# Output projection of two attention layers in column groups of 256, 256 and 512 instead of 512 and 512

## The chip, the cores and the metric

The kernel runs on one core of one Trainium2 chip. The metric is the time of one execution on the device, in microseconds (us); the time before is the median of 3 runs, 1074.47 us (1072.22 to 1074.48). The engines of the core are called PE (TensorE, matrix products), DVE (VectorE), ACT (ScalarE), POOL (GpSimd) and SP (SyncE, which issues the loads).

## What is computed

A trunk of four residual layers over 512 tokens of width 1024 in float32: a gated short convolution, a sparse attention, a latent attention and once more the convolution. Each layer is x + Mixer(RMSNorm(x)). What the change touches is the last line of the two attentions, the product of the gated attention output (512 x 1024) with a 1024 x 1024 matrix:

```python
def reference(x, positions, ...):
    for i in range(DEPTH):                       # DEPTH = 4
        kind, j = i % N_MIXERS, i // N_MIXERS    # 0 conv, 1 sparse, 2 latent, 0 conv
        ...
        x = x + y

def dsa_mixer(xn, positions, w_in, q_norm, k_norm, w_out):
    q, k, v, z, qi, ki, wi = jnp.split(xn @ w_in, cuts, axis=-1)
    ...                                          # top-k keys per query, 16 heads of 64
    p = jax.nn.softmax(logits, axis=-1)
    o = jnp.einsum("qhk,qkhd->qhd", p, v_sel)
    ...
    return (o * jax.nn.silu(z)) @ w_out

def mla_mixer(...):
    ...                                          # 16 heads, chunk-causal softmax attention
    return (o * jax.nn.silu(z)) @ w_out
```

## The kernel before

The residual stream lies transposed in SBUF, as eight tiles `X[k]` of 128 features x 512 tokens. A float32 product is made of three matmuls on operands split in two (`hi`, `lo`): `products` (L274 to L276) issues hi x hi, lo x hi and hi x lo. The weights come from HBM as `raw` tiles (three buffers), are split by `convert` (ACT writes `whi`, L153, then POOL writes `wlo`, L155) into four buffers each, and are used once per bank of the group of columns that they belong to.

`features` computes one group of output columns: for each k-tile of 128 input features it issues three matmuls into each of the group's PSUM banks (128 output features x 512 tokens per bank), and when the last k-tile is done, `finish` takes the banks away; for the output projection that is `residual`, which adds a bank to its `X[f]` on DVE. `project_out` goes through the column groups of a projection and asks `banks_of` for four banks per group. There are eight banks: two with the tag `pj` (projections), two with `pt` (turned probabilities), a double one with the tag `s` (scores), and one each with `o` (the mix of probabilities and values) and `tr` (transposes). A weight tile of a group of 512 columns holds one k-tile, one of 256 columns holds two (`Group.per`), so each conversion covers 128 x 512 elements in either case. One projection is 8 k-tiles x 8 blocks x 3 = 192 matmuls named `po`.

The attentions go over eight pairs of heads, and each pair over four blocks of 128 queries, in the steps `scores` (PE into the `s` banks, then DVE masks them and takes the extreme `mn`, L622, ACT takes the exponentials, L625), `normalise` (POOL for one head of the pair, L640, ACT for the other, L642), `turn` (PE transposes into `pt`, L652, ACT or DVE copies back, L657, L655) and `mix` (PE into `o`, L673). A `Filler` lets PE do projections of later pairs between these steps; the last of it are the gate columns 6 and 7, whose products (`pz`) use the `pj` banks. The mix of pairs 0 to 5 is multiplied by its gate on the way out of PSUM; pairs 6 and 7 go to `plain` and are multiplied on POOL when their gates are there (L890, L1066). Then `branch_out` splits the eight gated tiles into `xh` and `xl` (L715, L716) and calls `project_out`. Its eight k-tiles are the eight pairs, so k-tiles 6 and 7 wait for the last two pairs.

The program is written in this order, but a scheduler places the instructions on each engine by its own simulated timeline: a `po` product may stand between steps of the attention if its operands and its bank are free by then. On the chip each engine takes its instructions in the order of this list and waits for semaphores.

Of the kernel before, what the change touches and what calls it, by code (L numbers as in the profile page):

```python
# [69 lines left out]
def encoder(ctx: ExitStack, tc: tile.TileContext, a, out, depth=4):  # L70
# [23 lines left out]
    def bank(name, tag):  # L94
        return ps.tile([P, S], F32, name=name, tag=tag, bufs=BANKS[tag])

    def two_banks(name):

        b = ps.tile([P, 2, S], F32, name=name, tag="s", bufs=1)
        return [b[:, 0], b[:, 1]]  # L100

    def banks_of(name, which):

        if which % 2 == 0:
            return [bank(name, "pj") for _ in range(2)] + two_banks(name)
        return [bank(name, tag) for tag in ("pt", "pt", "o", "tr")]
# [113 lines left out]
    def run(*gens):  # L220
        for g in gens:
            for _ in g:
                pass
# [62 lines left out]
    def features(group, act, finish, banks):  # L286

        for k0, u in units(group):
            for j, w in enumerate(u):
                k = k0 + j  # L290
                x = act(k)
                for i, b in enumerate(banks):
                    c = i * P
                    n = min(P, group.n - c)
                    products(b[:n], [t[:, c:c + n] for t in w], x, k == 0, k == group.nk - 1)
            yield
        for i, b in enumerate(banks):
            finish(i, b)
# [118 lines left out]
    def residual(f, b, last):  # L417
        if last:
            o = wk("out")
            dve.tensor_tensor(o, b, X[f], op=OP.add)  # L420
            nc.sync.dma_start(out[:, f, :], o)
        else:
            dve.tensor_tensor(X[f], b, X[f], op=OP.add)

    def project_out(groups, act, last=False):
        f = 0
        for i, g in enumerate(groups):
            nb = g.n // P
            banks = banks_of("po", i + 1) if nb == 4 else [bank("po", ["pj", "pt"][i % 2])]
            run(features(g, act, lambda j, b, f=f: residual(f + j, b, last), banks))  # L430
            f += nb


    def layer_a(j, last):
# [35 lines left out]
        for f in range(8):  # L470
# [7 lines left out]
            if f == 1 and j == 0 and depth > 1:  # L478
                TAB["sc"] = angles()
        project_out(a[f"a_out{j}"], lambda k: G[k], last)  # L480


# [226 lines left out]
    def branch_out(groups, G, last):  # L709

        act = []
        for x in G:
            hi = tile_of("xh", "xh", dtype=F32R)
            lo = tile_of("xl", "xl", dtype=F32R)
            act_e.activation(hi, x, AF.Copy)  # L715
            dve.tensor_tensor(lo, x, hi.bitcast(F32), op=OP.subtract)  # L716
            act.append((hi, lo))
        project_out(groups, lambda k: act[k], last)
# [381 lines left out]
def _rows(w, cols):  # L1100

    w = w[:, cols]
    return np.ascontiguousarray(w.reshape(w.shape[0] // P, P, w.shape[1]).transpose(1, 0, 2))


def _cols(v):
    return v.reshape(-1, P).T


def pack(inputs):  # L1110
    f = {k: np.asarray(v) for k, v in inputs.items()}
    arr = {}
    arr["x"] = _rows(f["x"][0].T, slice(None))
    arr["pos"] = np.ascontiguousarray(f["positions"][0].reshape(NT, P).T)
    arr["inv"] = np.ascontiguousarray(np.broadcast_to(np.array(INV, np.float32), (P, 32)))
    arr["ident"] = np.eye(P, dtype=np.float32)
    conv = [_cols(np.ascontiguousarray(f["a_conv_w"][j])) for j in range(2)]
    arr["gains"] = np.ascontiguousarray(np.concatenate(
        [_cols(f["a_norm"][0]), _cols(f["b_norm"][0]), _cols(f["c_norm"][0]), _cols(f["a_norm"][1]),
         conv[0], conv[1], _cols(f["a_conv_b"][0]), _cols(f["a_conv_b"][1]),  # L1120
         _cols(f["c_q_lat_norm"][0]), _cols(f["c_kv_lat_norm"][0])], axis=1))
    arr["rows"] = np.concatenate([f["b_q_norm"][0], f["b_k_norm"][0], f["c_q_norm"][0], f["c_k_norm"][0]])[None]
    groups = {}

    def put(name, w, cols):
        arr[name] = _rows(w, cols)
        return name

    def outs(name, w, last=False):
        g = [put(f"{name}_0", w, slice(0, 512))]  # L1130
        if last:
            return g + [put(f"{name}_1{j}", w, slice(512 + P * j, 640 + P * j)) for j in range(4)]
        return g + [put(f"{name}_1", w, slice(512, 1024))]

    for j in range(2):
        w = f["a_w_in"][j]
        groups[f"a_in{j}"] = [
            put(f"a_in{j}_{i}", w, np.concatenate([np.arange(P) + D * b + P * i for b in range(4)]))
            for i in range(8)]
        groups[f"a_out{j}"] = outs(f"a_out{j}", f["a_w_out"][j], last=j == 1)  # L1140
    w = f["b_w_in"][0]
    for n, c in (("q", 0), ("k", 1024), ("v", 2048)):
        groups["b_" + n] = [put(f"b_{n}_{i}", w, slice(c + 256 * i, c + 256 * i + 256)) for i in range(4)]
    groups["b_z"] = [put(f"b_z_{i}", w, slice(3072 + P * i, 3200 + P * i)) for i in range(8)]
    groups["b_idx"] = [put("b_idx_0", w, slice(4096, 4416)), put("b_idx_1", w, slice(4416, 4680))]
    w = f["c_w_in"][0]
    cq = np.arange(384)
    groups["c_lat"] = [put("c_lat_0", w, np.concatenate([np.arange(384, 640), cq[:256]])),
                       put("c_lat_1", w, np.concatenate([cq[256:], np.arange(640, 672)]))]
    groups["c_z"] = [put(f"c_z_{i}", w, slice(672 + P * i, 800 + P * i)) for i in range(8)]  # L1150
    groups["c_uq"] = [put(f"c_uq_{i}", f["c_w_uq"][0], slice(384 * i, 384 * i + 384)) for i in range(4)]
    groups["c_ukv"] = [put(f"c_ukv_{i}", f["c_w_ukv"][0], slice(512 * i, 512 * i + 512)) for i in range(4)]
    groups["c_out"] = outs("c_out", f["c_w_out"][0])
    groups["b_out"] = outs("b_out", f["b_w_out"][0])
    return arr, groups


# [25 lines left out]
```

## Time and profile before

| | us |
|---|---|
| median of 3 runs (lowest to highest) | 1074.47 (1072.22 to 1074.48) |
| the profiled execution, its own time | 1078.64 |
| its span, first to last instruction | 1076.9 |
| PE busy | 1053.8 |
| POOL busy | 690.2 |
| DVE busy | 522.1 |
| ACT busy | 512.1 |
| mean granted clock of PE | 0.99 of 2.4 GHz |

A busy PE is not PE at its full rate: the clock may be granted at half. Layer 0 (convolution) takes the first 227 us, the sparse attention up to 575 us, the latent attention up to 855 us, and the last convolution the rest.

### The profile page before, as it was taken

To read this page: it belongs to the slowest core of one execution; us is meant where nothing else is said; L and a number is where in the kernel's file an instruction comes from. 1 tells how busy PE (TensorE), PEld (TensorE's weight loads), DVE (VectorE), ACT (ScalarE), POOL (GpSimd) and SP (SyncE) were. 2 spreads that over 40 slices of the span, in tenths; PEclk is the share of its full clock that TensorE was granted. 3 is DMA by queue.
4 is the path that set the end of the run, shared out by engine and by line. 5 is a ranking of instruction groups with operands and counts; after the bars stand their busy time and mean duration, and the time that the engine had idled before them with its cause. 6 is when DMAs were issued, how large, how long until landed. Compare 5 with 4: busy or idle time off the path is not lost.

```text
span 1076.9 us, 16214 instructions
## 1 busy us (share of the span) xinstructions
PE 1053.8 (98%) x6044; PEld 883.4 (82%) x6044; DVE 522.1 (48%) x1063; ACT 512.1 (48%) x1081; POOL 690.2 (64%) x636
## 2 busy tenths in 40 slices
PE   8999999999999999999899999999989999999998
PEld 6888888898898999998688777788758888888887
DVE  7784234336598974445423243444541463344221
ACT  5343323433444466767544447876762433333331
POOL 5646555667378899685375589697834665555552
PEclk9999999999999999999899999999988999999999
DMA  6333333223212221112032211111201333333332
GB/s 219 89 115 95 98 94 94 82 77 119 79 60 98 65 75 60 60 40 61 20 97 83 71 65 50 40 42 60 74 5 59 98 98 98 97 97 91 98 100 85
DMA packets 26574, 86.43 MB, mean 80 GB/s; under 512 B 3328, under 2 KB 4224, under 8 KB 26496
## 3 DMA queue, kind: packets, MB, share of 16 engines
q1 hardware_dynamic: 26352, 85.36, 25.4%
q8 instruction: 47, 0.77, 0.3%
q14 instruction: 31, 0.25, 0.1%
q10 hardware_dynamic: 144, 0.05, 0.0%
HBM read 83.30 MB, written 2.10 MB: 79 GB/s over the span
## 4 chain that ended last, share of the span: by engine, by line
PE 90%; DVE 3%; ACT 2%; POOL 2%; issue 1%; DMA 1%; SPq 0%; DVEq 0%; ACTq 0%; POOLq 0%
PE pa L275 10%; PE pa L276 10%; PE pa L274 10%; PE po L274 6%; PE po L276 5%; PE po L275 5%; PE o L673 3%; PE pt L652 3%; PE s L1050 3%; PE pz L276 2%; PE pz L274 2%; PE pz L275 2%; PE s L283 2%; PE tr L552 2%; PE pq L274 2%; PE pk L275 1%
## 5 line engine op out<-in xcount | busy, mean ns | idle before, releaser
L155 POOL TENSOR_TENSOR wlo<-raw,whi 128x512 fp32r<-128x512 f32 (+4 forms) x315 | 401.8, 1282 | 251.2 <-ACT whi L153 241.9
L153 ACT ACTIVATE whi<-raw 128x512 fp32r<-128x512 f32 (+4 forms) x319 | 195.3, 617 | 351.5 <-PE pa L275 162.4
L275 PE MATMUL pa<-xl,whi 128*128 128x512 f32 x512 | 199.5, 390 | 1.0 <-DVE xl L347 1.0
L274 PE MATMUL pa<-xh,whi 128*128 128x512 f32 x512 | 198.5, 390 | 0.5 <-ACT xh L346 0.5
L276 PE MATMUL pa<-xh,wlo 128*128 128x512 f32 x512 | 197.3, 389 | 0.0
L275 PEld LDWEIGHTS pa<-xl,whi 128*128 128x128 f32 x512 | 96.1, 188 | 21.5 <-DVE xl L347 2.0
L274 PEld LDWEIGHTS pa<-xh,whi 128*128 128x128 f32 x512 | 95.9, 188 | 21.1 <-ACT xh L346 1.1
L276 PEld LDWEIGHTS pa<-xh,wlo 128*128 128x128 f32 x512 | 96.1, 188 | 20.1
L640 POOL TENSOR_SCALAR p<-p,rc 128x128 f32<-128x128 f32 (+1 forms) x64 | 69.3, 1088 | 52.2 <-DVE rc L635 52.0
L625 ACT ACTIVATE p<-p,mn 128x128 f32<-128x128 f32 (+3 forms) x128 | 71.0, 558 | 19.5 <-DVE mn L622 19.4
L447 DVE TENSOR_TENSOR cg<-pa,R 128x512 f32<-128x512 f32 x16 | 11.0, 690 | 130.2 <-PE pa L276 129.0
L652 PE MATMUL pt<-ident,p 128*128 128x128 f32 x320 | 51.9, 289 | 3.7 <-ACT p L657 2.0
L622 DVE CUSTOM_DVE_ANT_0 p<-s,cmask,qs 128x128 f32<-128x128 f32 (+2 forms) x80 | 37.9, 506 | 32.0 <-PE s L1050 19.7
L652 PEld LDWEIGHTS pt<-ident,p 128*128 128x128 f32 x320 | 38.7, 147 | 16.0 <-issue 7.7
L274 PE MATMUL po<-xh,whi 128*128 128x512 f32 x128 | 51.7, 404 | 0.1
L274 PE MATMUL pz<-xh,whi 128*128 128x512 f32 x128 | 51.1, 399 | 0.3 <-ACT whi L153 0.3
L276 PE MATMUL pz<-xh,wlo 128*128 128x512 f32 x128 | 50.9, 399 | 0.1
L347 DVE SCALAR_TENSOR_TENSOR xl<-x,gains,xh 128x512 fp32r<-128x512 f32 x32 | 42.5, 1356 | 17.1 <-ACT xh L346 16.8
L275 PE MATMUL po<-xl,whi 128*128 128x512 f32 x128 | 50.6, 395 | 0.0
L275 PE MATMUL pz<-xl,whi 128*128 128x512 f32 x128 | 50.4, 393 | 0.0
L657 ACT ACTIVATE p<-pt 128x384 f32<-128x384 f32 (+1 forms) x80 | 39.1, 508 | 22.8 <-PE pt L652 22.7
L269 POOL TENSOR_TENSOR y<-mean,minus_half 128x16 f32<-128x16 f32 (+1 forms) x18 | 49.4, 2746 | 0.6
(243 smaller groups left out, 2454.8 us busy)
## 6 DMA issues: line engine op xcount, KB each, us to landing
raw<-in_a_in SPq DMA_DIRECT2D x63, 512.0 KB, 3.9
raw<-in_a_out SPq DMA_DIRECT2D x16, 512.0 KB, 3.9
raw<-in_b_z SPq DMA_DIRECT2D x8, 512.0 KB, 3.5
raw<-in_b_q SPq DMA_DIRECT2D x8, 512.0 KB, 3.4
raw<-in_b_k SPq DMA_DIRECT2D x8, 512.0 KB, 3.5
raw<-in_b_v SPq DMA_DIRECT2D x8, 512.0 KB, 3.7
raw<-in_b_out SPq DMA_DIRECT2D x8, 512.0 KB, 4.0
raw<-in_c_z SPq DMA_DIRECT2D x8, 512.0 KB, 3.6
```

Of the source, the lines that this page charges most:

```text
L153: act_e.activation(hi, raw[:, j:j + m], AF.Copy)
L155: e.tensor_tensor(out=lo, in0=raw[:, j:j + m], in1=hi.bitcast(F32), op=OP.subtract)
L269: pool.tensor_tensor(out=y, in0=m, in1=minus_half[:, :n], op=OP.pow)
L274: nc.tensor.matmul(o, l[0], r[0], start=first, stop=False)
L275: nc.tensor.matmul(o, l[0], r[1], start=False, stop=False)
L276: nc.tensor.matmul(o, l[1], r[0], start=False, stop=last)
L347: dve.scalar_tensor_tensor(lo, X[k], g, hi.bitcast(F32), op0=OP.mult, op1=OP.subtract)
L622: dve.tensor_tensor_reduce(out=p[:, w], in0=banks[e][:, w], in1=j["masks"](t), scale=j["qs"](e, t), scalar=-GONE, op0=OP.add, op1=OP.min, ...
L625: act_e.activation(p[:, w], p[:, w], AF.Exp, bias=mn[e][:, i:i + 1], scale=-1.0, accum_out=sm[:, e * n + i:e * n + i + 1])
L640: pool.tensor_scalar(p[:, w], p[:, w], rc[:, i:i + 1], None, op0=OP.mult)
L652: pe.transpose(b[:, i:i + P], p[:, i:i + P], ident)
L657: act_e.activation(p[:, :n], b[:, :n], AF.Copy)
```

## The change

The output matrices of both attentions are cut into column groups of 256, 256 and 512, not 512 and 512. The first group of 256 goes to the two `pj` banks, the second to the double `s` bank, the group of 512 to `pt`, `pt`, `o` and `tr`. Before, the first 512 columns went to `pt`, `pt`, `o`, `tr` and the other 512 to `pj`, `pj` and `s`. The projections of the convolutions keep their groups. The diff is whole:

```diff
@@ project_out
         f = 0
         for i, g in enumerate(groups):
             nb = g.n // P
-            banks = banks_of("po", i + 1) if nb == 4 else [bank("po", ["pj", "pt"][i % 2])]
+            if nb == 4:
+                banks = banks_of("po", i + 1)
+            elif nb == 2:
+                banks = [bank("po", "pj") for _ in range(2)] if f == 0 else two_banks("po")
+            else:
+                banks = [bank("po", ["pj", "pt"][i % 2])]
             run(features(g, act, lambda j, b, f=f: residual(f + j, b, last), banks))
             f += nb
@@ pack
-    def outs(name, w, last=False):
+    def outs(name, w, last=False, halves=False):
+        if halves:
+            return [put(f"{name}_{c}", w, slice(c, d)) for c, d in ((0, 256), (256, 512), (512, 1024))]
         g = [put(f"{name}_0", w, slice(0, 512))]
...
-    groups["c_out"] = outs("c_out", f["c_w_out"][0])
-    groups["b_out"] = outs("b_out", f["b_w_out"][0])
+    groups["c_out"] = outs("c_out", f["c_w_out"][0], halves=True)
+    groups["b_out"] = outs("b_out", f["b_w_out"][0], halves=True)
```

The new lines move later line numbers by five: L652 of before is L657 of the changed kernel, L673 is L678, L1050 is L1055. Where the instructions stand is seen in the order of each engine. The names: `po` output projection, `s` scores (6 matmuls per tile width in the sparse attention, 2 in the latent one), `pt` transposes of probabilities, `o` the mix (the row counts one of two halves), `xh`, `xl` the split attention output, `whi`, `wlo` the split weights.

The first place is PE at the end of the sparse attention (layer 1), from just ahead of the first scores of pair 7 (`s` of 128 columns) on. Before:

```order
L652 MATMUL pt<-ident,p 128x128 x3
L283 MATMUL s<-kT,qT 128x128 x6
L283 MATMUL s<-kT,qT 128x256 x6
L283 MATMUL s<-kT,qT 128x384 x6
L652 MATMUL pt<-ident,p 128x128 x8
L283 MATMUL s<-kT,qT 128x512 x6
L652 MATMUL pt<-ident,p 128x128 x3
L673 MATMUL o<-p,v 64x128 x20
L652 MATMUL pt<-ident,p 128x128 x17
```

With the change, where these rows follow on 15 + 19 other `po` matmuls since the last gate product (before 8 + 1 + 3):

```order
L275 MATMUL po<-xl,whi 128x512
L276 MATMUL po<-xh,wlo 128x512
L283 MATMUL s<-kT,qT 128x128 x6
L283 MATMUL s<-kT,qT 128x256 x6
L657 MATMUL pt<-ident,p 128x128 x8
L283 MATMUL s<-kT,qT 128x384 x6
L678 MATMUL o<-p,v 64x128 x20
L657 MATMUL pt<-ident,p 128x128 x4
L283 MATMUL s<-kT,qT 128x512 x6
L657 MATMUL pt<-ident,p 128x128 x8
```

The scores of pair 7 now follow on 36 `po` matmuls instead of 12, eight transposes and the mix stand between them, and behind the last transposes of this piece (the 128- to 384-wide ones) stand 36 `po` matmuls, then the transposes of the 512-wide ones, 18 more `po`, and the last mix. Before, all transposes stood together, and 12 `po` matmuls ahead of the last mix.

The second place is PE at the end of the latent attention (layer 2), from pair 6's last scores to the last transposes. Before:

```order
L275 MATMUL po<-xl,whi 128x512
L276 MATMUL po<-xh,wlo 128x512
L652 MATMUL pt<-ident,p 128x128 x6
L1050 MATMUL s<-kT,qT 128x512 x2
L652 MATMUL pt<-ident,p 128x128 x6
L1050 MATMUL s<-kT,qT 128x128 x2
L1050 MATMUL s<-kT,qT 128x256 x2
L1050 MATMUL s<-kT,qT 128x384 x2
L652 MATMUL pt<-ident,p 128x128 x11
L1050 MATMUL s<-kT,qT 128x512 x2
L673 MATMUL o<-p,v 64x128 x20
L652 MATMUL pt<-ident,p 128x128 x17
```

With the change:

```order
L275 MATMUL po<-xl,whi 128x512
L276 MATMUL po<-xh,wlo 128x512
L657 MATMUL pt<-ident,p 128x128 x6
L1055 MATMUL s<-kT,qT 128x128 x2
L1055 MATMUL s<-kT,qT 128x256 x2
L1055 MATMUL s<-kT,qT 128x384 x2
L657 MATMUL pt<-ident,p 128x128 x8
L1055 MATMUL s<-kT,qT 128x512 x2
L657 MATMUL pt<-ident,p 128x128 x3
L678 MATMUL o<-p,v 64x128 x20
L657 MATMUL pt<-ident,p 128x128 x6
L274 MATMUL po<-xh,whi 128x512
```

The twelve `po` matmuls that ended above the transposes of pair 6 are gone from there: 30 stand now further up, ahead of pair 6's 384-wide scores, and 6 behind its 512-wide scores, of which the last two are the first rows here. Pair 7's 128-, 256- and 384-wide scores follow each other as before. Behind its last scores and mix begin 54 `po` matmuls, with the remaining transposes among them, before the last mix of the layer (before: 12).

The third place is ACT at the end of the sparse attention, from pair 6's 512-wide exponentials (`p,sum`) to pair 7's first. Before:

```order
L625 ACTIVATE p,sum<-p,mn 128x512
L657 ACTIVATE p<-pt 128x384
L625 ACTIVATE p,sum<-p,mn 128x512
L642 ACTIVATE p<-p,rc 128x512
L625 ACTIVATE p,sum<-p,mn 128x128
L625 ACTIVATE p,sum<-p,mn 128x256
L625 ACTIVATE p,sum<-p,mn 128x128
L625 ACTIVATE p,sum<-p,mn 128x256
```

With the change:

```order
L630 ACTIVATE p,sum<-p,mn 128x512
L153 ACTIVATE whi<-raw 128x512
L630 ACTIVATE p,sum<-p,mn 128x512
L153 ACTIVATE whi<-raw 128x512
L647 ACTIVATE p<-p,rc 128x512
L662 ACTIVATE p<-pt 128x384
L153 ACTIVATE whi<-raw 128x512
L630 ACTIVATE p,sum<-p,mn 128x128
L662 ACTIVATE p<-pt 128x512
L630 ACTIVATE p,sum<-p,mn 128x256
L630 ACTIVATE p,sum<-p,mn 128x128
L630 ACTIVATE p,sum<-p,mn 128x256
```

Three conversions of weights (`whi`) stand now between the exponentials. Before, ACT converted the next weights of the projection only after both `xh` of `plain`.

## Rows read from the trace of the kernel before

**Rows 1.** The page of the profile: the span, PE's line of busy time (us, share, instructions), the granted clock in 40 slices of the span (tenths of full speed) and the chain that ended last, by engine.

```profile
span 1076.9 us, 16214 instructions
...
PE 1053.8 (98%) x6044; PEld 883.4 (82%) x6044; DVE 522.1 (48%) x1063; ACT 512.1 (48%) x1081; POOL 690.2 (64%) x636
...
PEclk9999999999999999999899999999988999999999
...
PE 90%; DVE 3%; ACT 2%; POOL 2%; issue 1%; DMA 1%; SPq 0%; DVEq 0%; ACTq 0%; POOLq 0%
```

**Rows 2.** The table of stages, one line per stretch (us from the span's start): length, then busy us and instructions of each engine, the granted clock of PE, the share of the DMA engines, GB/s. The first stretch is the end of layer 1, the third the end of layer 2, each down to the next layer's first matmul; the second, fourth and fifth lie in them.

```profile
508.39:575.17 66.78, 63.24 (x383) 51.09 (x382) 24.59 (x52) 33.37 (x70) 34.73 (x27) 0.95 0.20 64
520.36:527.18 6.82, 6.49 (x46) 5.02 (x46) 3.11 (x10) 4.04 (x10) 2.75 (x3) 0.50 0.01 4
775.92:855.00 79.08, 74.33 (x408) 58.40 (x407) 26.18 (x60) 38.19 (x85) 37.24 (x31) 0.91 0.18 54
793.43:800.25 6.82, 6.48 (x17) 4.29 (x18) 2.48 (x9) 4.53 (x15) 2.28 (x4) 0.50 0.00 0
807.08:813.90 6.82, 6.35 (x19) 5.09 (x20) 1.38 (x2) 0.65 (x2) 0.41 (x1) 0.50 0.00 0
855.00:1036.00 181.00, 181.00 (x800) 149.85 (x799) 80.47 (x92) 58.91 (x97) 102.03 (x76) 1.00 0.31 96
```

**Rows 3.** The timeline of PE in layer 1 from 513 to 537 us: start, us, line, operation; in brackets how long PE stood idle before the row, and whose result ended that.

```profile
513.20 0.96 PE L283 MATMUL s<-kT,qT 64*128 64x512 f32 x6
...
516.29 0.95 PE L283 MATMUL s<-kT,qT 64*128 64x128 f32 x12 [0.29 <-DVE mn L622]
...
519.00 0.79 PE L283 MATMUL s<-kT,qT 64*128 64x384 f32 x6 [1.76 <-DVE mn L622]
...
521.50 1.65 PE L283 MATMUL s<-kT,qT 64*128 64x512 f32 x6 [0.33 <-DVE mn L622]
...
529.69 1.78 PE L652 MATMUL pt<-ident,p 128*128 128x128 f32 x11 [1.01 <-ACT p L657]
...
534.59 2.40 PE L673 MATMUL o<-p,v 128*64 128x128 f32 x40
```

**Rows 4.** The same in layer 2 from 782 to 817 us.

```profile
782.46 1.56 PE L1050 MATMUL s<-kT,qT 96*128 96x384 f32 x4
...
790.66 1.58 PE L1050 MATMUL s<-kT,qT 96*128 96x128 f32 x8 [0.86 <-DVE mn L622]
793.77 2.93 PE L1050 MATMUL s<-kT,qT 96*128 96x384 f32 x4 [1.53 <-DVE mn L622]
...
805.31 0.55 PE L652 MATMUL pt<-ident,p 128*128 128x128 f32 x3 [0.66 <-ACT p L657]
807.55 1.97 PE L652 MATMUL pt<-ident,p 128*128 128x128 f32 x8 [1.70 <-POOL p L640]
...
814.41 2.40 PE L673 MATMUL o<-p,v 128*64 128x128 f32 x40
```

**Rows 5.** The timeline of PE elsewhere: eight transposes and what follows them, two `po` matmuls behind a mix, and the first of two successive `po` products (three matmuls lie from one row to the other).

```profile
484.19 1.09 PE L652 MATMUL pt<-ident,p 128*128 128x128 f32 x8
485.04 0.36 PE L274 MATMUL pv<-whi,xh 128*128 128x256 f32 x1
...
536.92 0.50 PE L274 MATMUL po<-xh,whi 128*128 128x512 f32 x1
537.26 0.40 PE L275 MATMUL po<-xl,whi 128*128 128x512 f32 x1
...
853.64 0.39 PE L274 MATMUL po<-xh,whi 128*128 128x512 f32 x1
...
854.32 0.39 PE L274 MATMUL po<-xh,whi 128*128 128x512 f32 x1
```

**Rows 6.** The timeline of DVE: the first and the last of four passes over the first scores of pair 7 in layer 1, the two over its 512-wide scores, the copy and the split of the last `plain`, and the two over the 384-wide scores of pair 6 in layer 2.

```profile
517.52 0.34 DVE L622 CUSTOM_DVE_ANT_0 p<-s,cmask,qs 128x128 f32<-128x128 f32 x1
...
518.46 0.48 DVE L622 CUSTOM_DVE_ANT_0 p<-s,mask,qs 128x256 f32<-128x256 f32 x1
...
525.92 0.75 DVE L622 CUSTOM_DVE_ANT_0 p<-s,mask,qs 128x512 f32<-128x512 f32 x1 [2.76 <-PE o L673]
...
526.60 0.74 DVE L622 CUSTOM_DVE_ANT_0 p<-s,mask,qs 128x512 f32<-128x512 f32 x1
...
537.04 0.69 DVE L680 COPY plain<-o 128x512 f32<-128x512 f32 x1 [4.17 <-PE o L673]
...
539.80 0.69 DVE L716 TENSOR_TENSOR xl<-plain,xh 128x512 fp32r<-128x512 f32 x1 [2.07 <-ACT xh L715]
...
784.06 0.62 DVE L622 CUSTOM_DVE_ANT_0 p<-s,cmask,qs 128x384 f32<-128x384 f32 x1 [0.76 <-PE s L1050]
...
785.20 0.61 DVE L622 CUSTOM_DVE_ANT_0 p<-s,cmask,qs 128x384 f32<-128x384 f32 x1
```

**Rows 7.** The timelines of ACT and POOL in layer 1: a conversion on each, then `xh` of the last `plain` and the next conversions on ACT.

```profile
508.36 0.63 ACT L153 ACTIVATE whi<-raw 128x512 fp32r<-128x512 f32 x1 [0.37 <-PE pz L275]
...
509.12 1.29 POOL L155 TENSOR_TENSOR wlo<-raw,whi 128x512 fp32r<-128x512 f32 x1 [0.96 <-ACT whi L153]
...
539.13 0.63 ACT L715 ACTIVATE xh<-plain 128x512 fp32r<-128x512 f32 x1 [7.05 <-POOL plain L890]
540.47 2.67 ACT L153 ACTIVATE whi<-raw 128x512 fp32r<-128x512 f32 x4 [0.70 <-PE po L275]
```

## The prediction, made before the changed kernel ran

> **What bounds the kernel now.** I read the page first. TensorE (PE) is busy for 1053.8 of 1076.9 us and holds 90% of the chain that ended last; its granted clock, in tenths, is 9 in 37 of 40 slices and 8 in three, one just before the middle and two around slice 30 [rows 1]. So time can come from two things: PE standing still, and PE at half clock. The table of stages says where both are. I cut it from the first `po` matmul of the sparse attention to the first matmul of the next layer (b, 66.78 us), and from the last gate matmul of the latent attention to the next layer (c, 79.08 us). PE stands still for 66.78 - 63.24 = 3.54 us in b and 79.08 - 74.33 = 4.75 us in c. Three stretches of 6.82 us lie in them at a granted clock of 0.50, that is 1.2 instead of 2.4 GHz, busy for 6.49, 6.48 and 6.35 us: at full clock this work takes half, so they cost 3.25, 3.24 and 3.18 us. After c, to 1036, PE is busy throughout at 1.00 [rows 2]. What this change can reach is therefore 3.54 + 3.25 = 6.8 us in b and 4.75 + 6.42 = 11.2 us in c, 18.0 us in all.
>
> The timeline of PE shows what it waits for. In b the scores of the last pair wait for VectorE (0.29, 1.76 and 0.33 us, released by `mn`), the last transposes for ScalarE (1.01) [rows 3]. In c it is 0.86 and 1.53 us for `mn`, then 0.66 for ScalarE and 1.70 for GpSimd [rows 4]. This is the end of an attention: the softmax of the last two pairs runs on the other engines, and PE has nothing else to do, although 192 matmuls of the output projection stand behind it. Only four products (12 matmuls) of these come before the last pair and 12 more before the last mix, because one bank is free for them (`tr`), and the four weight buffers then stay held by products whose banks are not.
>
> **The change, part by part.** Work on PE: the same 192 matmuls of 512 columns per layer and the same 16 conversions, of 128x512 elements each; nothing is added or removed. One matmul takes 0.68 / 3 = 0.227 us in a row [rows 5].
>
> Order on PE, layer b: before the last pair's scores there are now 36 `po` matmuls, not 12 (six k-tiles into the two `pj` banks), then 36 + 18 more between the last scores and the last mix, not 12. A fill of 24 x 0.227 = 5.4 us goes in front of the waits of 0.29 and, with the eight transposes put between, of 1.76; one of 54 x 0.227 = 12.3 us covers the chain that ended with 1.01. What is left I get from VectorE. Its four passes over the first scores of the last pair run from 517.52 to 518.94, 1.42 us, its two over the 512-wide ones from 525.92 to 527.34, 1.42 us [rows 6]. In front of the 384-wide scores stand now only eight transposes, 0.85 us (as from 484.19 to 485.04 in an earlier pair [rows 5]), so with the way to VectorE and back about 0.7 us of wait stays; the second projection group, which needs the score banks empty, stands behind eight transposes likewise: 0.7 us. With 0.2 for latencies, 1.6 us. Bounds: nothing, and the 3.54 of today. The first product into the second `pj` bank waits for the last gate's evacuation, but follows it by some 5 us; I cost it at nothing. Two more turns between transposes and `po` cost 0.1 us each (0.34 instead of 0.23 after a mix [rows 5]). So b: 63.24 - 3.25 + 1.6 + 0.2 = 61.8 us, 5.0 less, if the clock stays up.
>
> Layer c: 30 of the 36 early matmuls (6.8 us) go in front of the 384-wide scores of pair 6, where PE is already full; that shifts the rest and gains nothing by itself. They are taken from two places. Twelve stood behind those scores and hid VectorE's passes over them (784.06 to 785.81, 1.75 us [rows 6]); only six transposes stand there now, so a new wait of about 0.9 us is in front of the 512-wide scores. Six stand behind these and take the place of the wait of 0.86. The wait of 1.53 is not touched: the last pair's 128-, 256- and 384-wide scores still follow each other with nothing between. In front of its 512-wide scores stand eight transposes instead of eleven, and they ran at half clock: about 0.5 us of wait is new. Then 54 matmuls (12.3 us) cover 0.66 and 1.70. Idle: 0.9 + 1.6 + 0.5 = 3.0 us, between 1.5 (the row that is not touched) and 4.75. `po` now stands in eleven pieces instead of three: eight or nine turns at 0.1, 0.9 us. So c: 74.33 - 6.42 + 3.0 + 0.9 = 71.8 us, 7.3 less.
>
> Other engines: conversions move forward into the softmax, three in b in front of the last pair's first exponentials, each 0.63 us of ScalarE and 1.29 us of GpSimd [rows 7]. Each waits until PE has freed a weight buffer, and the exponentials queue behind it. By the steps above the first buffer of b comes free some 2 us after the 512-wide scores of pair 6, as ScalarE is through with the first half of their exponentials, and the third just ahead of the last pair's scores, which its exponentials need anyway. I cost the three at nothing; without that cover they cost 3 x 0.63 = 1.9 us a layer. The last mix's chain (`plain`, gate product, `xh`, `xl`) takes 3.6 us by before's rows, 536.92 to 540.49 [rows 6, 7]; 18 `po` matmuls (4.1 us) that need none of it stand ahead. SyncE's queue is the same. The next layer's first products go into `pj` and score banks that are now empty earlier, but PE did not wait there before: nothing.
>
> Sum: 5.0 + 7.3 = 12.3 us, against the profiled execution's own time of 1078.64 us (span 1076.9 and 1.74 around it): 1066.3. The median of the runs shown is 4.17 us below that execution. If that is the profiling, the changed kernel comes to 1074.47 - 12.3 = 1062.2; if the unprofiled runs lose one half-clock stretch fewer, there is 3.2 us less to win: 1065.4. I say 1063.5.
>
> **The rivals.** *The clock still falls in c.* For it: before each of its two falls PE had stood still for 0.86 + 1.53 and 0.66 + 1.70 us [rows 4], and 1.6 + 0.5 us close together is what I leave. Against: no wait over 1.7 us is left, and the one of 1.76 in b was the longest before. A stretch costs 3.2 us: 1066.7. The Trainium skill, "TensorE: Matmul & The Clock Gate", section "A second HAM failure mode: psum-queue depth-cycling", says that short idle moments between groups of matmuls that cycle through banks can be enough to make the clock swing, and this change makes more groups and cycles more banks. The trace neither bears that out nor excludes it: the falls here follow waits for other engines, not turns between banks.
>
> *The chain sets the end, not PE.* What is put ahead of the last pair's scores delays them by 5.4 us, and fills PE only if the softmax behind it then overlaps the 54 later matmuls. If a part of the conversions holds ScalarE up, half of the gain goes: 6 us, 1068.5.
>
> *No change.* The new waits (up to 4.75 - 1.5 in c) and the clock take all back: 1074.
>
> *Slower.* Place: ScalarE's queue. From pair 6 on, six conversions per layer wait for PE to free a buffer while PE waits for exponentials queued behind them. That ScalarE holds to its order the trace shows: `whi` at 540.47 stands behind an `xh` that waited 7.05 us [rows 7]. Each such knot stops PE for what the exponentials take from there; with 12 knots it decides from (12.3 + 2.1) / 12 = 1.2 us each, and at 1.5 us, two exponentials, the kernel takes 1074.5 - 12.3 + 18 = 1080. Against: in the order, the buffer that each needs is freed by PE matmuls that do not depend on what is behind it. The Trainium skill says the same of the queue ("PSUM — Partial Sum Buffer", section "Engine vs sequencer instructions": ScalarE's is strictly first in, first out), and the trace agrees.
>
> **How the numbers follow.** Forecast 0.50 (1061 to 1066), the clock falls in c 0.25 (1065 to 1068), half the gain 0.12 (1068 to 1071), no change 0.06, slower 0.07. Were PE never to wait in either tail, another 4.6 us would go: 1058.9. The range from 1058.5 to 1069.5 takes in the first two and half of the third. Within 0.2% of before (2.1 us, about what a measurement of this kernel can tell from nothing) lies only the fourth: faster 0.87, same 0.06, slower 0.07.
>
> **What would show it.** In b the waits for `mn` in the last pair under 1 us each, none for ScalarE before the last transposes, and a granted clock of 1.00 throughout. In c a wait of about 1.5 us before the 384-wide scores of the last pair as today, new ones of 0.9 and 0.5 before two 512-wide scores, none after the last of these. From the first `po` or last gate matmul to the next layer 62 and 72 us. Wrong it would be if ScalarE's exponentials of the last pair start late behind a conversion, if the clock falls, or if PE waits for `wlo` after the last mix.

## The result, and the profile of the changed kernel

The changed kernel takes 1063.24 us (median of 4 executions, 1063.14 to 1063.29, all four at a granted clock of 1.00), the kernel before 1074.47 (1072.22 to 1074.85): 11.2 us less, a ratio of 0.9899 with a 95% interval of 0.9884 to 0.9914. Measured twice more beside the experiments, it gains 9.9 and 9.6 us, ratios of 0.9912 (0.9894 to 0.9929) and 0.9908 (0.9886 to 0.9929); six of those ten executions were at 0.998 (below).

The page of the profile; these lines answer to [rows 1]:

```profile
span 1061.4 us, 16210 instructions
...
PE 1044.5 (98%) x6044; PEld 877.0 (83%) x6044; DVE 531.7 (50%) x1063; ACT 511.7 (48%) x1081; POOL 695.2 (66%) x636
...
PEclk9999999999999999999999999999999999999999
...
PE 90%; DVE 3%; POOL 3%; ACT 2%; issue 1%; DMA 1%; SPq 0%; DVEq 0%; POOLq 0%
```

The three slices at 8 are gone. PE has as many matmuls as before and is busy 9.3 us less, about what the three stretches at half clock had cost it (9.67). The table of stages for the two tails, with the columns and boundaries of [rows 2] (first output product, or the row behind the last gate product, to the next layer's first matmul):

```profile
507.04:567.74 60.70, 59.94 (x383) 48.67 (x382) 25.83 (x52) 32.96 (x70) 35.49 (x27) 1.00 0.23 70
768.55:839.50 70.95, 68.35 (x409) 53.96 (x407) 27.61 (x60) 38.21 (x85) 38.57 (x31) 1.00 0.20 60
```

The tail of layer 1 (b) is 6.08 us shorter than before, that of layer 2 (c) 8.13. The spans differ by 15.5; what is left lies ahead of b, which begins at 508.39 before and at 507.04 now, though PE's order up to there is the same; the kernel before itself reaches b at 507.26 in another execution (base_again, below). PE now stands still for 0.76 us in b (before 3.54) and 2.60 in c (before 4.75). The timeline of PE shows all of it, first b, then c; against [rows 3, 4]:

```profile
520.07 0.96 PE L283 MATMUL s<-kT,qT 64*128 64x128 f32 x12
520.96 1.09 PE L657 MATMUL pt<-ident,p 128*128 128x128 f32 x8
522.57 0.79 PE L283 MATMUL s<-kT,qT 64*128 64x384 f32 x6 [0.51 <-DVE mn L627]
...
527.78 0.94 PE L657 MATMUL pt<-ident,p 128*128 128x128 f32 x6 [0.24 <-POOL p L645]
528.70 0.50 PE L274 MATMUL po<-xh,whi 128*128 128x512 f32 x1
...
542.12 2.40 PE L678 MATMUL o<-p,v 128*64 128x128 f32 x40
544.45 0.50 PE L274 MATMUL po<-xh,whi 128*128 128x512 f32 x1
```

```profile
785.21 1.98 PE L1055 MATMUL s<-kT,qT 96*128 96x512 f32 x4 [0.68 <-DVE mn L627]
...
789.06 1.48 PE L1055 MATMUL s<-kT,qT 96*128 96x128 f32 x8
792.07 1.56 PE L1055 MATMUL s<-kT,qT 96*128 96x384 f32 x4 [1.53 <-DVE mn L627]
793.47 1.04 PE L657 MATMUL pt<-ident,p 128*128 128x128 f32 x8
794.89 1.98 PE L1055 MATMUL s<-kT,qT 96*128 96x512 f32 x4 [0.38 <-DVE mn L627]
```

In b the eight transposes stand in front of the 384-wide scores and leave 0.51 of the wait of 1.76; the second projection group (528.70) starts without a wait. In c the wait of 1.53 is there as before, with smaller ones at the two 512-wide scores. The last mix (542.12) is followed at once by `po`.

### The profile page after: what moved, and what is told of

It reads as the page before. It is cut to its first block, busy times and chain, and to the rows that moved or that the text cites. A ratio compares the mean times of both kernels' runs of the same rounds, so it can differ in the third digit from the quotient of the medians.

```text
span 1061.4 us, 16210 instructions
## 1 busy us (share of the span) xinstructions
PE 1044.5 (98%) x6044; PEld 877.0 (83%) x6044; DVE 531.7 (50%) x1063; ACT 511.7 (48%) x1081; POOL 695.2 (66%) x636
## 4 chain that ended last, share of the span: by engine, by line
PE 90%; DVE 3%; POOL 3%; ACT 2%; issue 1%; DMA 1%; SPq 0%; DVEq 0%; POOLq 0%
PE pa L276 10%; PE pa L275 10%; PE pa L274 10%; PE po L274 6%; PE po L275 5%; PE po L276 5%; PE o L678 3%; PE pt L657 3%; PE s L1055 3%; PE pz L276 2%; PE pz L274 2%; PE pz L275 2%; PE s L283 2%; PE tr L557 2%; PE pq L274 2%; PE pk L275 1%
## 5 line engine op out<-in xcount | busy, mean ns | idle before, releaser
L452 DVE TENSOR_TENSOR cg<-pa,R 128x512 f32<-128x512 f32 x16 | 11.1, 691 | 123.5 <-PE pa L276 121.2
L657 PE MATMUL pt<-ident,p 128*128 128x128 f32 x320 | 49.2, 277 | 0.6 <-ACT p L662 0.3
L275 PE MATMUL po<-glo,whi 128*128 128x512 f32 x128 | 49.8, 389 | 0.0
L274 PE MATMUL po<-ghi,whi 128*128 128x512 f32 x128 | 49.5, 389 | 0.0
```

Of the source, the lines that this page charges most:

```text
L274: nc.tensor.matmul(o, l[0], r[0], start=first, stop=False)
L275: nc.tensor.matmul(o, l[0], r[1], start=False, stop=False)
L657: pe.transpose(b[:, i:i + P], p[:, i:i + P], ident)
```

## The experiments

Each kernel was timed beside the kernel before on the same chip. The table gives, for a profiled execution of each, the length of the two tails, PE's standing still in them (length less busy time) and their granted clock.

| kernel | median us | before beside it | b: us, still, clock | c: us, still, clock |
|---|---|---|---|---|
| before, first profile | 1074.47 | | 66.78, 3.54, 0.95 | 79.08, 4.75, 0.91 |
| base_again | 1074.20 | 1074.46 | 64.86, 4.56, 1.00 | 76.28, 5.08, 0.96 |
| changed | 1063.24 | 1074.47 | 60.70, 0.76, 1.00 | 70.95, 2.60, 1.00 |
| sparse_only | 1069.22 | 1074.46 | 60.68, 0.75, 1.00 | 77.40, 4.76, 0.93 |
| latent_only | 1069.86 | 1074.46 | 66.74, 3.73, 0.95 | 70.90, 2.62, 1.00 |
| banks_only | 1065.97 | 1074.46 | 60.67, 0.84, 1.00 | 72.93, 4.31, 1.00 |
| cut_only | 1078.99 | 1074.16 | 69.05, 5.58, 0.95 | 76.62, 6.10, 0.98 |
| s_first | 1070.56 | 1074.16 | 65.98, 3.61, 0.95 | 72.14, 3.84, 1.00 |
| wide_384 | 1062.26 | 1074.16 | 59.95, 0.61, 1.00 | 68.39, 0.97, 1.00 |
| after_again (changed) | 1064.28 | 1074.16 | 60.66, 0.75, 1.00 | 70.96, 2.59, 1.00 |
| late_mn | 1064.68 | 1073.63 | 60.66, 0.75, 1.00 | 71.34, 2.99, 1.00 |
| fill_first | 1065.08 | 1073.63 | 60.66, 0.75, 1.00 | 72.85, 2.74, 0.98 |
| wide_c | 1061.85 | 1073.63 | 60.69, 0.76, 1.00 | 68.38, 0.97, 1.00 |
| after_third (changed) | 1064.07 | 1073.63 | 60.70, 0.75, 1.00 | 70.95, 2.60, 1.00 |

(In wide_384 and wide_c a few `po` matmuls stand behind the first matmul of the next layer; their tails are shorter by up to 0.9 us for that alone.)

**The kernel before once more (no edit).**

> The kernel before, unchanged, to see what its own executions differ by: the profiled one took 1078.64 us, the median of the others 1074.47, the lowest 1072.22, while the changed kernel's profiled execution and its others agree within 0.15 us. Theory A (the difference is the clock: the half-clock stretches of 6.82 us, 3.2 us each, do not all come in every execution, and the first loads vary by about 1 us): the executions lie on steps of some 3 us between about 1068 and 1079, and this profile shows two or three stretches at a granted clock of 0.50 in the two tails and a time that goes with their number. Theory B (taking the profile costs 4 us): the profiled execution lies above all others again, with the same three stretches.

Theory A. The profiled execution took 1072.89 us, below the median of its own twelve (1074.20; 1071.81 to 1077.57), so it is not the taking of a profile that costs 4 us. The executions' mean granted clock goes from 0.990 to 0.998 and the time with it: over the 29 spans measured in this comparison (12 here, 17 of the kernel before beside them), a straight line of the span against (1 - clock) x span has a slope of 0.70, and drawn on to a clock of 1.00, which none of them reached, it gives 1068.6. There are no clear steps of 3 us, as theory A had it. Stretches differ in length as well as in number: the profile of sparse_only (below) has one of some 3.4 us in c, from 787.3 to 790.7, and one of some 6.9, from 797.5 to 804.4. This profile has none in b and one in c. The table of stages of base_again, then its waits of PE in b and in c:

```profile
507.26:572.12 64.86, 60.30 (x383) 48.79 (x382) 24.60 (x52) 33.25 (x70) 34.76 (x27) 1.00 0.19 66
772.98:849.26 76.28, 71.20 (x408) 56.05 (x407) 26.19 (x60) 38.19 (x85) 37.22 (x31) 0.96 0.17 56
790.00:796.00 6.00, 5.16 (x15) 3.49 (x16) 2.61 (x12) 3.70 (x14) 2.32 (x3) 0.50 0.00 0
```

```profile
515.17 0.96 PE L283 MATMUL s<-kT,qT 64*128 64x128 f32 x12 [0.29 <-DVE mn L622]
517.88 0.79 PE L283 MATMUL s<-kT,qT 64*128 64x384 f32 x6 [1.75 <-DVE mn L622]
520.38 0.96 PE L283 MATMUL s<-kT,qT 64*128 64x512 f32 x6 [0.69 <-DVE mn L622]
526.66 1.78 PE L652 MATMUL pt<-ident,p 128*128 128x128 f32 x11 [1.68 <-ACT p L657]
```

```profile
787.73 1.58 PE L1050 MATMUL s<-kT,qT 96*128 96x128 f32 x8 [0.87 <-DVE mn L622]
790.84 2.93 PE L1050 MATMUL s<-kT,qT 96*128 96x384 f32 x4 [1.53 <-DVE mn L622]
802.08 0.55 PE L652 MATMUL pt<-ident,p 128*128 128x128 f32 x3 [0.66 <-ACT p L657]
804.33 1.09 PE L652 MATMUL pt<-ident,p 128*128 128x128 f32 x8 [1.71 <-POOL p L640]
```

The program, the order and the wait of 1.75 in b are those of [rows 3], where the clock fell. At full clock b is 64.86 us, not 66.78: a half-clock stretch cost 1.92 there, not the 3.25 that are half of PE's work in it, since the waits behind it shrink (0.33 instead of 0.69, 1.01 instead of 1.68). In c, one stretch less makes 2.80.

**One attention at a time.** The new cut in one layer, the old one in the other:

```diff
-    groups["c_out"] = outs("c_out", f["c_w_out"][0], halves=True)
+    groups["c_out"] = outs("c_out", f["c_w_out"][0])
```

> The change in the sparse attention alone; the latent attention keeps its two groups of 512. Theory 1 (each layer's gain is made in its own tail and the two add up): the tail of layer 1, from its first output product to the next layer, goes from 66.8 to about 60.7 us with a granted clock of 1.00, the tail of layer 2 keeps its half-clock stretches and its 79 us; 5 to 6.1 us less than before, 1068.4 to 1069.5. Rival (the tails are not independent: the first tail's order shifts what the second does, or its gain is given back in the latent attention): within 2 us of before, or within 2 us of the whole change (1063.2).

> The change in the latent attention alone. Theory 1: the tail of layer 2 goes from 79.1 to about 71.2 us without a half-clock stretch, waits of about 0.7, 1.5 and 0.4 us for VectorE left in it; the tail of layer 1 stays as before with its stretch; 6 to 7.9 us less than before, 1066.6 to 1068.5. Rival as for the change in the sparse attention alone.

(latent_only has the same edit at `b_out`.) Theory 1: 5.2 and 4.6 us less than before. The changed tail has the length that it has in the changed kernel, 60.68 and 70.90, the other stays as it was, stretches included: 77.40 and 66.74 us at 0.93 and 0.95. The gain in layer 2 came out below the 6 to 7.9 expected; that range was taken from a profile of before with two stretches in c. The two gains add up to 9.8 us, which is what the changed kernel gained in its two later measurements (9.9 and 9.6), and 1.4 less than in the first.

**The banks without the cut, the cut without the banks.** banks_only exchanges the banks of the two groups of 512:

```diff
-            banks = banks_of("po", i + 1) if nb == 4 else [bank("po", ["pj", "pt"][i % 2])]
+            banks = banks_of("po", i + 1 - swap) if nb == 4 else [bank("po", ["pj", "pt"][i % 2])]
...
-        project_out(groups, lambda k: act[k], last)
+        project_out(groups, lambda k: act[k], last, swap=1)
```

> Two groups of 512 columns as before, but the banks exchanged: the first 512 columns go to pj, pj and the double s bank, the other 512 to pt, pt, o and tr. Nothing is cut. In the order, 24 output products stand before the last pair's scores in layer 1 (36 with the change, 12 before) and 53 between the last scores and the last mix (54 with the change, 12 before); in layer 2 also eight transposes and the mix stand between the last pair's scores. Theory 1 (it is the banks: products that need only banks free during the last softmax stand ready): both tails keep a granted clock of 1.00 and the time is that of the change within 2 us, 1062 to 1065. Rival (it is the cut: a weight tile of 256 columns is used up in two banks, so that the four weight buffers turn over, while one of 512 stays held for the s banks): about half of the gain, 1068 to 1071, with waits for VectorE and half-clock stretches left in the tails.

cut_only keeps the groups of 256, 256 and 512 and puts them on the old banks:

```diff
-                banks = banks_of("po", i + 1)
+                banks = banks_of("po", i + (i != 2))
...
-                banks = [bank("po", "pj") for _ in range(2)] if f == 0 else two_banks("po")
+                banks = [bank("po", tag) for tag in (("pt", "pt") if f == 0 else ("o", "tr"))]
```

> The cut into 256, 256 and 512 columns without the new banks: the groups of 256 on pt, pt and on o, tr, the group of 512 on pj, pj and the double s bank. In the order no output product stands ahead of the last pair's scores or between them (before 12, with the change 36 in layer 1), and 19 or 20 between the last scores and the last mix (before 12, with the change 54). Theory 1 (it is the banks): no gain; the waits and the half-clock stretches of before stay, and the twelve products that went ahead are missing: 1073 to 1077. Rival (weight tiles that are used up in two banks are enough): 1071 or less.

The banks alone bring 8.5 us, most of the gain, though the time lies 1 us above theory 1's range; the cut alone costs 4.8, 2 us above its range there, and PE stands still longer than in base_again in both tails (5.58 and 6.10 us beside 4.56 and 5.08). In b the exchange is all there is to gain (60.67 beside 60.70). In c it leaves 4.31 us of standing still, the cut 1.7 less. The waits of PE in c of banks_only:

```profile
784.83 1.98 PE L1050 MATMUL s<-kT,qT 96*128 96x512 f32 x4 [0.69 <-DVE mn L622]
788.19 0.88 PE L652 MATMUL pt<-ident,p 128*128 128x128 f32 x6 [1.38 <-POOL p L640]
791.15 1.09 PE L652 MATMUL pt<-ident,p 128*128 128x128 f32 x8 [0.77 <-POOL p L640]
800.59 0.50 PE L274 MATMUL po<-xh,whi 128*128 128x512 f32 x1 [1.47 <-DVE mn L622]
```

The last row is what the rival spoke of: the next product needs an s bank, which VectorE has not emptied. Where 36 matmuls of the changed kernel go to pj ahead of the last pair's softmax, four weight tiles of 512 columns allow 24 (four tiles, two free banks, three matmuls each).

**Only the fill behind the last scores.** The two groups of 256 exchanged. Here and in the next two kernels a list names the banks of each group, and the columns are cut by the same list; the edits are shown against the kernel before, in s_first for `b_out` (`c_out` has the same):

```diff
-        branch_out(a["b_out"], gate[:6] + plain, last)
+        branch_out(a["b_out"], gate[:6] + plain, last, [('s', 's'), ('pj', 'pj'), ('pt', 'pt', 'o', 'tr')])
```

> The change with its two groups of 256 exchanged: the first on the s banks, the second on pj. The four weight buffers are then held by the group that waits for s, so no output product goes ahead of the last pair's scores in either layer, and all of the fill (67 products in layer 1, 65 in layer 2) lies between the last scores and the last mix. Theory 1 (both fills are worth their waits): layer 1 keeps its waits for VectorE of 0.3, 1.8 and about 0.7 us before the last pair's scores, so 2 us of idle more than the change, and a half-clock stretch with them in most executions; layer 2 waits 0.9 and 1.5 us as before, about what the change leaves there, with a stretch in some; the waits for ScalarE and GpSimd before the last transposes are gone: 1065.5 to 1069. Rival (only the fill behind the last scores counts): within 1 us of the change.

Theory 1 for the mechanism, but 1.6 us above its range. In b the waits of before for `mn` stand ahead of the last pair's first two groups of scores, with a half-clock stretch, and there is a new wait of 1.02 us ahead of the mix at 509.09, where nine of before's twelve early matmuls stood, which are missing too. In c PE stands still for 3.84 us at a clock of 1.00, 1.2 more than with the change. Its waits in b:

```profile
509.09 2.40 PE L678 MATMUL o<-p,v 128*64 128x128 f32 x40 [1.02 <-DVE p L660]
513.50 0.55 PE L657 MATMUL pt<-ident,p 128*128 128x128 f32 x3 [0.31 <-ACT p L662]
514.52 0.95 PE L283 MATMUL s<-kT,qT 64*128 64x128 f32 x12 [0.47 <-DVE mn L627]
517.28 1.33 PE L283 MATMUL s<-kT,qT 64*128 64x384 f32 x6 [1.81 <-DVE mn L627]
```

**More fill: columns of 384, 256 and 384.** The first group on pj, pj and tr, in both layers (wide_384) or in the latent attention alone (wide_c):

```diff
-        branch_out(a["c_out"], gate[:6] + plain, last)
+        branch_out(a["c_out"], gate[:6] + plain, last, [('pj', 'pj', 'tr'), ('s', 's'), ('pt', 'pt', 'o')])
...
-    groups["c_out"] = outs("c_out", f["c_w_out"][0])
+    groups["c_out"] = outs("c_out", f["c_w_out"][0], plan=[('pj', 'pj', 'tr'), ('s', 's'), ('pt', 'pt', 'o')])
```

> Column groups of 384, 256 and 384: the first on pj, pj and tr, the second on the double s bank, the third on pt, pt and o. Half as many products again can go ahead of the last softmax. In the order of layer 2, 18 products stand now around the transposes ahead of pair 6's 512-wide scores, 12 behind these, and eight transposes ahead of pair 7's 384-wide scores; in layer 1, 18 more stand ahead of the last pair's 384-wide scores. Theory 1 (TensorE's order is all): the waits of 0.68, 1.53 and 0.38 us that the change leaves in layer 2 go for the most part, and the 0.51 in layer 1; 2 to 2.5 us less idle, half a microsecond for turns: 1061 to 1062. Rival (conversions in ScalarE's queue cost after all: five stand ahead of the last pair's first exponentials in layer 1, not three): TensorE waits for exponentials of the last pair, 1064 or more.

> Columns of 384, 256 and 384 in the latent attention alone, those of the change in the sparse one. Theory 1 (the wider first group gains by the fill ahead of the last pair's scores in layer 2, where the change left 2.6 us of waiting; layer 1 had less than 1 us left): the time of the variant with 384 in both layers, 1061.8 to 1062.7, granted clock 1.00 in every execution. Rival (the gain was in layer 1, or in both): halfway to the changed kernel or above.

Theory 1 for the mechanism in both: 1062.26 beside 1064.28 for the changed kernel, though 0.3 above the range of 1061 to 1062, and 1061.85 beside 1064.07, within its range. Some of these 2 us is the clock: against the changed kernel's executions at 1.00 (1063.3 on average, below) they gain 1.0 and 1.4, and standing still in c falls by 1.6. wide_c has the lowest time of all kernels here, at 0.9887 of before (0.9867 to 0.9906); from wide_384 (0.9894, 0.9878 to 0.9911) it can't be told apart, so the wider group adds nothing in layer 1 that these runs show. Its waits in c are two, 0.97 us together, and none for an exponential ahead of the last scores:

```profile
793.98 1.04 PE L657 MATMUL pt<-ident,p 128*128 128x128 f32 x8
795.68 1.56 PE L1055 MATMUL s<-kT,qT 96*128 96x384 f32 x4 [0.66 <-DVE mn L627]
...
802.74 0.55 PE L657 MATMUL pt<-ident,p 128*128 128x128 f32 x3 [0.31 <-ACT p L662]
```

**The changed kernel's own clock.** Beside these it ran again:

> The changed kernel, unchanged, on the same chip as the others: 1063.0 to 1063.5, a granted clock of 1.00 in every execution. Theory A of the base's executions (the spread of before is the half-clock stretches) says that its executions agree within 0.5 us; if they spread by more, the spread has another cause.

> The changed kernel once more, beside the three above: 1063.0 to 1063.5 where its clock stays at 1.00, about 1.9 us more in the executions at 0.998. If the profile falls on one of these, it shows the place: theory 1 says in layer 2 between the waits of 1.53 and 0.38 us; the rival that it is elsewhere (start or end of the kernel).

It does not stay at 1.00. Of its 14 executions in all, eight show 1.00 and take 1063.3 on average (1062.98 to 1063.67), six 0.998 and 1064.5. Two kernels tried the wait of 1.53 us as the cause. late_mn makes it longer by a copy on VectorE, fill_first has a larger copy, to which the order answers by moving eight transposes ahead of the waiting scores:

```diff
+                if c == 42 and e == 1 and "late" in jobs[0]:
+                    dve.tensor_copy(p[:, :192], banks[1][:, :192])
...
```

> The changed kernel with one copy of 128x192 more on VectorE, between its passes over the last pair's first scores in layer 2 (the copy's result is overwritten). TensorE's order is that of the change to the last row; the wait of 1.53 us before the last pair's 384-wide scores becomes about 1.9. The question is why two of four executions of the changed kernel showed a mean granted clock of 0.998 and took 1.9 us longer. Theory 1 (it is a half-clock stretch in layer 2, and a longer wait there brings it in more executions): most executions at 0.997 or 0.998, median 1065 to 1066.5. Rival (it comes independently of these waits): as many executions at 1.00 as of the changed kernel beside it, and 0.4 us more than that.

> The same with a copy of 128x256. It costs VectorE about 0.5 us, but the order answers to it: eight transposes (0.85 us) now stand ahead of the last pair's 384-wide scores in layer 2, as they do in layer 1, and the mix ahead of its 512-wide scores. Theory 1: the wait before the 384-wide scores falls from 1.53 to about 1.1 us, that of 0.38 goes; 0.8 us less idle, and no execution below a granted clock of 1.00: 1062.2 to 1063. Rival (the late VectorE pass puts the whole last softmax back by what it takes): not below the changed kernel beside it.

(fill_first copies 256 columns instead of 192; `late` is set for the latent attention alone.) late_mn lengthens the wait as meant:

```profile
792.31 1.56 PE L1057 MATMUL s<-kT,qT 96*128 96x384 f32 x4 [1.93 <-DVE mn L629]
```

Three of six executions are at 0.998, beside four of six of the changed kernel: no more than without it. Its executions at 1.00 take 0.5 us more than those of the changed kernel, as the rival has it. That a longer wait brings the stretch more often is not borne out, though six executions are few. fill_first went against theory 1: 1.0 us slower than the changed kernel beside it, and five of six executions at 0.998 or 0.999. Its profile caught a stretch. The timeline of PE in c, then a window in that stretch:

```profile
789.03 1.48 PE L1057 MATMUL s<-kT,qT 96*128 96x128 f32 x8
792.31 1.59 PE L659 MATMUL pt<-ident,p 128*128 128x128 f32 x8 [1.81 <-POOL p L647]
793.70 2.69 PE L1057 MATMUL s<-kT,qT 96*128 96x384 f32 x4
```

```profile
793.00:796.00 3.00, 3.00 (x9) 1.94 (x8) 0.87 (x2) 1.41 (x5) 1.50 (x2) 0.50 0.00 0
```

The transposes put in as fill were themselves not ready: they wait 1.81 us for GpSimd, in the place of the scores' 1.53, and the clock falls behind that wait. In wide_c the same eight transposes in the same place waited for nothing; twelve `po` matmuls, not six, stand there between pair 6's last scores and them, which is 1.4 us (six times 0.227) more for GpSimd. That a stretch of the changed kernel lies there too is not shown: all three of its profiles fell on executions at 1.00. Nor is it settled why one execution falls and the next does not.

## Why the prediction came out right

The time was 1063.24 where 1063.5 was forecast, by the mechanism named: the waits went as the order said, and the stretches at half clock went with them. That the two numbers lie 0.3 us apart is in part luck. The terms of the sum had the wrong sizes and made up for each other, and the first four executions all kept their clock, which six of the later ten did not (1064.28 and 1064.07).

**Order and waits.** Right, wait by wait. In b 0.51 us for `mn` where 0.7 stood; the second 0.7, ahead of the group on the score banks, did not come, 0.24 for GpSimd came instead; none for ScalarE before the last transposes. In c 0.68, 1.53 and 0.38 where 0.9, 1.5 and 0.5 stood, and none after. The tails are 60.7 and 71.0 us where 62 and 72 stood.

**Turns.** Over-sized: PE's work in c at full clock was 67.91 (74.33 - 6.42) and is 68.35, so 0.4 us and not 0.9; in b nothing and not 0.2 (59.94 now, 60.30 in base_again at full clock).

**Conversions at nothing.** Held. No wait of PE in either tail ends on ScalarE. Of the three conversions ahead of the last pair's exponentials in b only the third waits for PE to free its buffer, 0.20 us, and the first exponential behind it then waits for its own `mn`, not for ScalarE:

```profile
519.94 0.63 ACT L153 ACTIVATE whi<-raw 128x512 fp32r<-128x512 f32 x1 [0.20 <-PE po L275]
521.47 0.40 ACT L630 ACTIVATE p<-p,mn 128x128 f32<-128x128 f32 x1 [0.89 <-DVE mn L627]
```

In all of b ScalarE waits so 9 times and 11.1 us by the table of waits, all but these 0.20 behind those exponentials:

```profile
ACT whi L153 <- PE po L275: 11.1, 9, 2.1
```

The rival of the knots falls with it, and so does the one that let the chain of ScalarE set the end. wide_384, with five conversions ahead of the last pair's first exponentials, agrees: PE waits for ScalarE in its b 0.25 us at a copy of transposes and 0.36 at an `xh`, and for no exponential. One reading under the knots was wrong: the `whi` at 540.47 does not show that ScalarE holds to its order, for behind the `xh` it waited another 0.70 us for PE itself [rows 7]. The changed kernel shows it: in b ScalarE stands still for 0.30 us until PE's transposes let a copy start at 528.43, and the exponential that follows at 528.82 had had its `mn` since 527.97.

**The clock term, and what the waits were.** Here the sum had the wrong sizes. It took 3.25 us for b's stretch and 1.74 for its waits. base_again, which has b at full clock, shows 1.92 for the stretch (66.78 to 64.86) and 4.16 for the order (64.86 to 60.70; standing still 4.56 to 0.76). The waits had been read from a profile in which the half clock had shortened them. What one term had too much the other had too little, so the sum missed by less: 6.08 where 5.0 stood in b, 8.13 where 7.3 stood in c. In c 6.42 stood for two stretches and 0.85 for the order (4.75 - 3.0 - 0.9); base_again shows 2.80 for one stretch and leaves 5.33 (76.28 to 70.95) for the other and the order.

**From the profile to the median.** The profiled execution of before lies at the long end of that kernel's spread, with all three stretches and 1.35 us more ahead of b. Against it the change brings 15.5 us and not the 12.3 of the sum. Taking 12.3 off the median instead, on the thought that the profile had cost 4.17 us, was wrong in its reason (base_again's profiled execution lies below its median) and right in its size by luck. By an estimate from the line through the 29 spans, an average execution of before has less half-clock time to give back than the 9.67 us of the sum, some 4 us (median span 1072.7 less 1068.6 at clock 1.00), and more in its waits than 2.6 (1.74 + 0.85), some 7 (1068.6 less 1061.4).

**The clock falls in c.** This rival had 0.25, and the clock does fall in six of 14 executions, at 1.2 us and not 3.2; where, no profile shows. Every stretch that the traces of the other kernels have in b and c lies in a wait of 1.5 us or more for another engine, or shortly behind one. The rule that the prediction set beside it, that short idle moments between groups of matmuls that cycle through banks can be enough (the Trainium skill, "TensorE: Matmul & The Clock Gate", section "A second HAM failure mode: psum-queue depth-cycling"), is not what the profiles caught: wide_c takes as many groups through the banks and shows no stretch in either tail. For the six executions at 0.998 it is not excluded.

## What to carry to other kernels

When an engine is bound by a chain at the end of a stage, look for work whose inputs are ready but whose buffers are not: which bank comes free first decided 8.5 us here, of the 9.6 to 11.2 that the change brings, and the size of the piece only the rest. Ask of each piece put ahead of a wait whether it is itself ready there (fill_first's transposes were not). A profile that caught half-clock stretches shows waits that are too short and a clock that is too dear; take several executions of the kernel before, and cost both from one at full clock.

## What the runs showed of the hardware

One program in one order shows mean granted clocks from 0.990 to 0.998 from execution to execution, and 1071.8 to 1077.8 us with them. A wait of 1.76 us in b was followed by a half-clock stretch in one profile of before, and the same wait, 1.75 us, by none in another. A stretch of 6.8 us cost the kernel 1.92 us in b and 2.80 in c, less than half its length: behind the one in b the waits were 1.0 us shorter (standing still 3.54 instead of 4.56).
